# A hybrid attention, mLSTM and Hyena block on one core: new numbers in the estimate that orders TensorE's work

## The chip, the core and the metric

One NeuronCore of a Trainium2 chip runs the whole program: TensorE (PE in the rows) multiplies, VectorE (DVE), ScalarE (ACT) and GpSimd (POOL) work element by element, SyncE (SP) issues most transfers. The metric is the device time of one execution in microseconds. Each engine works through its own list of instructions in order and waits where an operand is not there yet.

## What is computed

Two layers, each of three mixers that read one projected input; the second layer does not update the context rows.

```python
def _layer(x, ctx, c, c_ctx, w_ada, ...):
    mod = jax.nn.silu(c) @ w_ada + b_ada            # shift, scale, gate
    h = _rmsnorm(x, g_pre) * (1.0 + scale) + shift  # 1024 rows; ctx has 256 more
    qa, ka, va, za, qm, km, vm, om, zm, gm, vh, x1h, x2h, zh = _split_cols(h @ w_in)
    o_na = _neighbourhood_attention(...)             # 8 heads, softmax over a window and the context
    h_lat, h_ctx = _mlstm_bidirectional(...)         # 4 heads, chunks with a carried state
    o_hy = _hyena(...)                               # two long convolutions by FFT
    y = concatenate([o_na * silu(za), sigmoid(om) * h_lat * silu(zm), o_hy * silu(zh)]) @ w_out
    return x + gate * _rmsnorm(y, g_post)
```

All arrays are float32. The kernel splits an operand of the large products into a high and a low part (names ending in hi and lo, h and l), so that one product is three matrix products.

## The kernel before, in words

Everything TensorE does is written by Python generators, called streams. A stream for each mixer emits its matmuls stage by stage and yields in between; one stream, `projections` (rank 2, the last to be chosen), emits the products of the input with `w_in`, 34 blocks of 128 columns and the gates per layer, each block in pieces of 512, 512 and 256 rows, each piece as 24 matmuls (names `pj`). The projections depend on little, so they are the filler: `flow` takes, at each step, the first stream by rank that is ready by the estimate, and where no mixer is ready it emits three `pj` matmuls.

What counts as ready is decided by class `Clock`. It keeps a planned time `now` for TensorE, and for every instruction that the kernel emits on another engine, and for every transfer, it books a planned duration on that engine (`run`) and notes when the result is there (`done`). A stream that yields tiles is not taken before their planned time plus 0.1 plus `margin` (0.3). So the order of TensorE's list is written out by this estimate; the order on the other engines is then made by the scheduling layer below, which follows the order in which instructions were emitted and lets nothing overtake a wait within an engine or within SP's queue. The estimate has no part in the running program.

The names the text needs. In the start: `htp` transposes the normed input, `tap`, `fs` make filters. Hyena (`h1`, `h2`, `h3`, `h4`: four products of the long convolution with stores to memory and loads back between them; `ztp`, `ctp` transposes; `c1`, `c2` the context's short convolution). mLSTM (`vtp`, `gtp`, `ktp` transposes, `mc`, `mst`, `mxe`, `mpi`, `mpn`, `mto`). Then neighbourhood attention, NA: 8 heads of 5 units (4 in layer 1). A unit is scores (`apl`, `apc`), a row maximum on DVE, exponentials on ACT, scaling on POOL and DVE (tile `ae`), transposes (`apt`), copies (`ph`), and, for two units together, the product with the values (`apo`); `avt` transposes values. Four `work` streams take units in turn. The loads of a head are `ark`, `arq` (keys, queries), `av` (values) and `ab` (bias, three buffers). In the names of instructions the first number is the layer, for NA then head and unit: `apl0_6_1` is layer 0, head 6, unit 1.

Last, `w_out`. `out_early` starts when the layer's projections or its NA are finished, in the memory that the projections' input gives free: it loads eight blocks (`wos`, 512 KB each, four buffers), splits them into `woh` (ACT) and `wol` (POOL, or POOL and DVE in turn once NA is over), and while NA is not finished it multiplies seven of the eight blocks for up to four row tiles (names `op`). `out_proj` does the rest, and for layer 0 its results are normed and transposed for the next layer (`htp1`).

Of the kernel before, what the change touches and what calls it, by code (L numbers as in the profile page):

```python
# [13 lines left out]
F32 = mybir.dt.float32  # L14
# [3 lines left out]
ALU = mybir.AluOpType  # L18
# [28 lines left out]

class Clock:

    RATE = dict(vector=(0.07, 1 / 960), scalar=(0.08, 1 / 1200), gpsimd=(0.2, 1 / 480))  # L50

    def __init__(self):
        self.now = 0.0
        self.runs, self.wrote, self.used, self.slots, self.home = {}, {}, {}, {}, {}

    @staticmethod
    def region(ap):
# [14 lines left out]
    def ready(self, aps):  # L72

        t = 0.0
        for ap in aps:
            name, r0, r1, c0, c1 = self.region(ap)
            for a0, a1, b0, b1, w in self.wrote.get(name, ()):
                if w > t and a0 <= r1 and r0 <= a1 and b0 <= c1 and c0 <= b1:
                    t = w
        return t  # L80

    def slot(self, ap):

        t = ap.tensor
        if ap.space == DRAM:
            return 0.0
        if t.name not in self.home:
            taken = self.slots.setdefault(t.tag, [])
            free = 0.0
            if len(taken) < t.tag_meta.bufs:  # L90
                taken.append(t.name)
            else:
                i = min(range(len(taken)), key=lambda i: self.used.get(taken[i], 0.0))
                free = self.used.get(taken[i], 0.0)
                taken[i] = t.name
            self.home[t.name] = free
        return self.home[t.name]
# [34 lines left out]
    def issue(self, engine, op, args, kw):  # L132
        outs = [kw[k] for k in ("out", "accum_out") if isinstance(kw.get(k), bass.AP)] or [args[0]]
        ins = [x for x in list(args) + list(kw.values()) if isinstance(x, bass.AP) and not any(x is o for o in outs)]
        t = max([self.now, self.ready(ins + [o for o in outs if o.space != DRAM])] + [self.slot(o) for o in outs])
        n = max(math.prod(x.shape[1:]) for x in outs + ins)
        if op == "dma_start":
            t = self.run("queue", 0.5, t + 0.2)
            end = self.run("dma", max(0.05, math.prod(outs[0].shape) * 4 / 360e3), t + 0.6) + 0.9
        else:  # L140
            fixed, per = self.RATE[engine]
            end = self.run(engine, fixed + n * per, t + 0.1)
        self.done(outs, ins, end)

# [16 lines left out]
class Kern:  # L161
# [16 lines left out]

    def mm(self, o, lhsT, rhs, start, stop, beside=False):

        n = 0 if beside else max(math.prod(o.shape[1:]), 128) * 4 if lhsT.dtype == F32 else max(math.prod(o.shape[1:]), 256)
        self.nc.tensor.matmul(o, lhsT=lhsT, rhs=rhs, start=start, stop=stop)  # L182
        self.pe(max(n / 2400.0, 0.06), o, [lhsT, rhs])

    def tr(self, out, in_, identity):
        self.nc.tensor.transpose(out=out, in_=in_, identity=identity)  # L186
        self.pe(out.shape[1] / 1200.0, out, [in_])

    def announce(self, what):
# [1851 lines left out]
```

## Time and profile before

| what | value |
|---|---|
| median of three runs | 1971.73 us (1970.43 to 1983.2) |
| the profiled execution | 1979.88 us, span 1978.0 us |
| PE busy | 1827.2 us, 92% of the span |
| granted TensorE clock, mean of the span | 0.968 |
| DVE, ACT, POOL busy | 53%, 39%, 23% |

PE is the engine that is nearly always busy. What is not its work is the time in which it is idle (151 us in all) and the time in which its clock is granted at half. Both are read by stage, since each stage has other waits.

### The profile page before, as it was taken

The page shows a single profiled execution, that of the slowest core. Times are in us where ns is not written, and L with a number is a line of the kernel's source. Part 1 is how long each engine was busy: PE and PEld are TensorE (multiplying, and loading weights), DVE is VectorE, ACT ScalarE, POOL GpSimd, SP SyncE. Part 2 cuts the span into 40 slices and gives each one's busy share as a digit, 9 for nine tenths or more (in the row PEclk, how much of TensorE's full clock was granted, in tenths as well). Part 3 has the DMA queues.
Part 4 walks back from the last instruction along what each step waited for, and adds up shares of the span by engine and source line. Part 5 has one row for each costly group of instructions (what it writes and reads, how often), then busy time and mean ns, then how long its engine had stood idle before and what let it go on. Part 6 is the DMA issues. An engine that isn't in the chain of part 4 may idle for free.

```text
span 1978.0 us, 28234 instructions
## 1 busy us (share of the span) xinstructions
PE 1827.2 (92%) x10008; PEld 1444.0 (73%) x10008; DVE 1054.5 (53%) x2402; ACT 780.2 (39%) x1517; POOL 457.7 (23%) x368
## 2 busy tenths in 40 slices
PE   8699988998999899999988998899899989999898
PEld 2365867787788677788877876678677767887776
DVE  3744353537735366677545534344762457777433
ACT  3645342414323244555343443332323145554321
POOL 1534120313220111212131123122412111222300
PEclk9799999999999999999998999899899999999999
DMA  8476887863221667655253457764222565554443
GB/s 314 140 246 219 277 229 229 232 231 97 89 81 46 197 188 217 206 163 160 96 189 98 148 170 209 205 195 168 77 79 82 156 196 146 161 170 132 159 148 107
DMA packets 233674, 328.91 MB, mean 166 GB/s; under 512 B 22573, under 2 KB 162249, under 8 KB 231614
## 3 DMA queue, kind: packets, MB, share of 16 engines
q1 hardware_dynamic: 182398, 247.67, 41.2%
q10 hardware_dynamic: 51136, 79.45, 11.8%
q8 instruction: 79, 1.29, 0.3%
q14 instruction: 61, 0.50, 0.1%
HBM read 230.82 MB, written 96.21 MB: 165 GB/s over the span
## 4 chain that ended last, share of the span: by engine, by line
PE 38%; DMA 6%; DVE 5%; issue 5%; ACT 2%; POOL 1%; SPq 0%; ACTq 0%; POOLq 0%; DVEq 0%
PE pj L182 15%; PE op L182 10%; PE apo L182 3%; PE apt L186 2%; PE h L182 2%; PE apl L182 1%; DMA wos<-in_wout 1%; PE apc L182 1%; DMA raw<-pr 1%; DVE u L155 1%; DMA pr<-sr 1%; PE mpn L182 1%; PE avt L186 1%; ACT ae L155 0%; POOL usw L155 0%
## 5 line engine op out<-in xcount | busy, mean ns | idle before, releaser
L182 PE MATMUL pj<-hhi,wh 128*128 128x512 f32 (+2 forms) x1504 | 599.4, 399 | 8.0 <-ACT sv L155 6.2
L182 PE MATMUL pj<-hlo,wh 128*128 128x512 f32 (+2 forms) x1504 | 554.1, 369 | 0.1
L182 PE MATMUL pj<-hhi,wl 128*128 128x512 f32 (+1 forms) x1456 | 538.8, 370 | 0.0
L182 PEld LDWEIGHTS pj<-hhi,wh 128*128 128x128 f32 (+1 forms) x1504 | 288.6, 192 | 61.7 <-issue 14.9
L182 PEld LDWEIGHTS pj<-hlo,wh 128*128 128x128 f32 (+1 forms) x1504 | 288.7, 192 | 47.6 <-issue 9.5
L182 PEld LDWEIGHTS pj<-hhi,wl 128*128 128x128 f32 x1456 | 280.3, 193 | 47.0
L155 POOL TENSOR_TENSOR wl<-wr,wh 128x1024 fp32r<-128x1024 f32 x68 | 163.7, 2407 | 547.9 <-ACT wh L155 473.0
L155 POOL TENSOR_SCALAR ae<-ae,ast 128x640 f32<-128x640 f32 (+1 forms) x72 | 68.2, 948 | 405.4 <-DVE ast L155 359.4
L155 ACT ACTIVATE ae<-ae,ast 128x640 f32<-128x640 f32 (+1 forms) x144 | 113.1, 787 | 85.6 <-DVE ast L155 82.2
L182 PE MATMUL op<-woh,yh 128*128 128x512 f32 x288 | 115.9, 402 | 8.9 <-ACT yh L155 8.9
L186 PE MATMUL apt<-ident,ae 128*128 128x128 f32 x672 | 101.8, 278 | 17.9 <-ACT ph L155 5.3
L182 PE MATMUL op<-woh,yl 128*128 128x512 f32 x288 | 114.4, 397 | 0.3 <-DVE yl L155 0.3
L182 PE MATMUL op<-wol,yh 128*128 128x512 f32 x288 | 114.6, 398 | 0.0
L155 ACT CAST wh<-wr 128x1024 fp32r<-128x1024 f32 (+1 forms) x70 | 71.9, 1028 | 102.3 <-PE pj L182 84.2
L155 ACT COPY sr<-pj 128x512 f32<-128x512 f32 (+3 forms) x94 | 49.2, 524 | 149.4 <-PE pj L182 141.7
L186 PEld LDWEIGHTS apt<-ident,ae 128*128 128x128 f32 x672 | 80.3, 142 | 33.8 <-issue 7.1
L155 ACT COPY ph<-apt 128x512 f32<-128x512 f32 (+1 forms) x136 | 65.0, 482 | 87.2 <-PE apt L186 82.3
L155 DVE CUSTOM_DVE_ANT_0 ae<-apl,ab 128x384 f32<-128x384 f32 x128 | 69.0, 552 | 36.2 <-PE apl L182 21.0
L182 PE MATMUL apo<-ph,aVn 128*64 128x256 f32 (+1 forms) x800 | 80.9, 350 | 0.4 <-ACT ph L155 0.4
L182 PEld LDWEIGHTS apo<-ph,aVn 128*64 128x64 f32 x800 | 51.9, 137 | 29.0 <-issue 8.8
L182 PEld LDWEIGHTS op<-woh,yh 128*128 128x128 f32 x288 | 55.7, 194 | 20.8 <-ACT yh L155 9.5
L155 DVE TENSOR_TENSOR yl<-gr,yh 128x1024 fp32r<-128x1024 f32 (+1 forms) x22 | 24.5, 1113 | 78.2 <-ACT yh L155 78.1
(255 smaller groups left out, 3058.6 us busy)
## 6 DMA issues: line engine op xcount, KB each, us to landing
wr<-in_wblk SPq DMA_DIRECT2D x68, 512.0 KB
ab<-in_nab SPq DMA_DIRECT2D x96, 192.0 KB
pr<-sr ACTq DMA_DIRECT2D x64, 256.0 KB
k<-ks SPq DMA_DIRECT2D x128, 128.0 KB
wada<-in_wada ACTq DMA_DIRECT2D x32, 512.0 KB
raw<-pr SPq DMA_DIRECT2D x20, 512.0 KB
ark<-pr SPq DMA_DIRECT2D x32, 320.0 KB
wada<-in_wada SPq DMA_DIRECT2D x16, 512.0 KB
```

What stands on the lines that cost most here:

```text
L155: r = emit(*args, **kw)
L182: self.nc.tensor.matmul(o, lhsT=lhsT, rhs=rhs, start=start, stop=stop)
L186: self.nc.tensor.transpose(out=out, in_=in_, identity=identity)
```

## The change

Only the numbers in `Clock` and the way it books a few things change. Fixed times of the vector, scalar and gpsimd engines go from 0.07, 0.08, 0.2 to 0.155, 0.165, 0.25 us, with an extra for results that are summed aside (`accum_out`) and for powers; a matmul is planned 9% longer (`PASS`), at least 0.12 us, and 0.15 us are added when the part of the array that is used changes (`turn`, `MODE`). A transfer ends 1.6 instead of 0.9 us after its bytes, at 300, 180 or 90 instead of 360 GB/s by the length of its rows, and a transfer that ACT issues takes planned time of ACT.

```diff
--- before.py
+++ after.py
@@ -47,11 +47,19 @@
 
 class Clock:
 
-    RATE = dict(vector=(0.07, 1 / 960), scalar=(0.08, 1 / 1200), gpsimd=(0.2, 1 / 480))
+
+    RATE = dict(vector=(0.155, 1 / 960, 0.08), scalar=(0.165, 1 / 1200, 0.19), gpsimd=(0.25, 1 / 478, 0.0))
+    POW = 0.3
+
+    PASS, MODE = 1.09, 0.15
+
+    LATENCY = 0.6, 1.6
+    SPEED = ((2048, 300e3), (512, 180e3), (0, 90e3))
 
     def __init__(self):
         self.now = 0.0
         self.runs, self.wrote, self.used, self.slots, self.home = {}, {}, {}, {}, {}
+        self.mode = None
 
     @staticmethod
     def region(ap):
@@ -78,6 +86,19 @@
                 if w > t and a0 <= r1 and r0 <= a1 and b0 <= c1 and c0 <= b1:
                     t = w
         return t
+
+    @staticmethod
+    def inner(ap):
+
+        run, out = 1, []
+        for stride, n in reversed(list(ap)):
+            if n == 1:
+                continue
+            if stride != run:
+                break
+            out.append((stride, n))
+            run *= n
+        return out
 
     def slot(self, ap):
 
@@ -135,10 +156,16 @@
         t = max([self.now, self.ready(ins + [o for o in outs if o.space != DRAM])] + [self.slot(o) for o in outs])
         n = max(math.prod(x.shape[1:]) for x in outs + ins)
         if op == "dma_start":
-            t = self.run("queue", 0.5, t + 0.2)
-            end = self.run("dma", max(0.05, math.prod(outs[0].shape) * 4 / 360e3), t + 0.6) + 0.9
+            t = self.run("queue" if engine == "sync" else engine, 0.4, t + 0.2)
+            row = 4 * min(math.prod(n for s, n in self.inner(x.ap)) for x in outs[:1] + ins[:1])
+            speed = next(v for k, v in self.SPEED if row >= k)
+            end = self.run("dma", max(0.05, math.prod(outs[0].shape) * 4 / speed), t + self.LATENCY[0]) + self.LATENCY[1]
         else:
-            fixed, per = self.RATE[engine]
+            fixed, per, side = self.RATE[engine]
+            if "accum_out" in kw:
+                fixed += side
+            if ALU.pow in kw.values():
+                fixed += self.POW
             end = self.run(engine, fixed + n * per, t + 0.1)
         self.done(outs, ins, end)
 
@@ -178,12 +205,21 @@
 
     def mm(self, o, lhsT, rhs, start, stop, beside=False):
 
-        n = 0 if beside else max(math.prod(o.shape[1:]), 128) * 4 if lhsT.dtype == F32 else max(math.prod(o.shape[1:]), 256)
+        n = 0 if beside else max(math.prod(o.shape[1:]), 128) * 4 if lhsT.dtype == F32 else max(math.prod(o.shape[1:]), 256) * Clock.PASS
         self.nc.tensor.matmul(o, lhsT=lhsT, rhs=rhs, start=start, stop=stop)
-        self.pe(max(n / 2400.0, 0.06), o, [lhsT, rhs])
+        self.turn(lhsT.shape[0], math.prod(lhsT.shape[1:]))
+        self.pe(max(n / 2400.0, 0.06 if beside else 0.12), o, [lhsT, rhs])
+
+    def turn(self, rows, columns):
+
+        mode = [next(s for s in (32, 64, 128) if n <= s) for n in (rows, columns)]
+        if self.clock.mode not in (None, mode):
+            self.clock.now += Clock.MODE
+        self.clock.mode = mode
 
     def tr(self, out, in_, identity):
         self.nc.tensor.transpose(out=out, in_=in_, identity=identity)
+        self.turn(in_.shape[0], math.prod(in_.shape[1:]))
         self.pe(out.shape[1] / 1200.0, out, [in_])
 
     def announce(self, what):
```

Every engine keeps the same work (TensorE's list has 7664 rows in both); what moves is the order. How many `pj` matmuls stand in TensorE's list ahead of some places:

| first instruction of | before | change |
|---|---|---|
| Hyena, layer 0 (h10_0_0_0) | 408 | 480 |
| mLSTM, layer 0 (vtp0_0_0) | 915 | 1212 |
| NA, layer 0 (apl0_0_0_0) | 1704 | 1992 |
| NA head 5, layer 0 (apl0_5_0_0) | 2058 | 2430 |
| NA head 7, layer 0 (apl0_7_0_0) | 2223 | 2496, all of the layer |
| Hyena, layer 1 (h11_0_0_0) | 2613 | 2616 |
| mLSTM, layer 1 (vtp1_0_0) | 3102 | 3249 |
| NA, layer 1 (apl1_0_0_0) | 3813 | 3936 |
| NA head 7, layer 1 (apl1_7_0_0) | 4239 | 4428, of 4464 |

Between mto0_1_2 and apl0_0_0_0 stand 111 `pj` before and 96 in the change; between mto1_1_1 and apl1_0_0_0 102 and 75.

TensorE's list in layer 1 around h41_0_0_0, the last product of the first long convolution, before:

```order
L182 MATMUL h31_1_0_1_11053<-pa1_1_0_1_10953,d2i_1_10481 128x512
L182 MATMUL pj1_31_0_11024<-hhi1_9506,wh1_31_10898 128x512
L182 MATMUL pj1_31_0_11024<-hlo1_9507,wh1_31_10898 128x512
L182 MATMUL pj1_31_0_11024<-hhi1_9506,wl1_31_10899 128x512
L182 MATMUL h21_1_0_3_11068<-t11_1_0_10769,d2_1_10479 128x512
L182 MATMUL pj1_31_0_11024<-hhi1_9506,wh1_31_10898 128x512
L182 MATMUL pj1_31_0_11024<-hlo1_9507,wh1_31_10898 128x512
L182 MATMUL pj1_31_0_11024<-hhi1_9506,wl1_31_10899 128x512
L182 MATMUL pj1_31_0_11024<-hhi1_9506,wh1_31_10898 128x512
L182 MATMUL pj1_31_0_11024<-hlo1_9507,wh1_31_10898 128x512
L182 MATMUL pj1_31_0_11024<-hhi1_9506,wl1_31_10899 128x512
L182 MATMUL h41_0_0_0_11083<-m1i_1_10477,s21_0_0_10987 128x64 x8
```

And the same place in the change (the run of `pj` ahead of h41_0_0_0 has 18 rows, its last six are shown):

```order
L209 MATMUL pj1_18_0_11227<-hhi1_9544,wh1_18_11129 128x512
L209 MATMUL pj1_18_0_11227<-hlo1_9545,wh1_18_11129 128x512
L209 MATMUL pj1_18_0_11227<-hhi1_9544,wl1_18_11130 128x512
L209 MATMUL pj1_18_0_11227<-hhi1_9544,wh1_18_11129 128x512
L209 MATMUL pj1_18_0_11227<-hlo1_9545,wh1_18_11129 128x512
L209 MATMUL pj1_18_0_11227<-hhi1_9544,wl1_18_11130 128x512
L209 MATMUL h41_0_0_0_11246<-m1i_1_10474,s21_0_0_11146 128x64 x8
```

More projections stand between the products of the convolution: 6 directly ahead of h41_0_0_0 before, 18 in the change, and the other channel's h21 and h31 have moved ahead of them.

TensorE's list in NA of layer 0, around the transposes of head 5, unit 2, before:

```order
L182 MATMUL apc0_5_4_8130<-kl0_5_7382,qs0_5_7381 128x256
L186 MATMUL apt0_5_2_0_8156<-ident_109,ae0_5_2_0_7979 128x128
L186 MATMUL apt0_5_2_0_8156<-ident_109,ae0_5_2_1_7996 128x128
L186 MATMUL apt0_5_2_0_8156<-ident_109,ae0_5_2_0_7979 128x128
L186 MATMUL apt0_5_2_0_8156<-ident_109,ae0_5_2_1_7996 128x128
L186 MATMUL apt0_5_2_1_8162<-ident_109,ae0_5_2_0_7979 128x128
L186 MATMUL apt0_5_2_1_8162<-ident_109,ae0_5_2_1_7996 128x128
L186 MATMUL apt0_5_2_1_8162<-ident_109,ae0_5_2_0_7979 128x128
L186 MATMUL apt0_5_2_1_8162<-ident_109,ae0_5_2_1_7996 128x128
L182 MATMUL pj0_32_1024_8168<-hhi0_373,wh0_32_7461 128x256
L182 MATMUL pj0_32_1024_8168<-hlo0_374,wh0_32_7461 128x256
L182 MATMUL pj0_32_1024_8168<-hhi0_373,wl0_32_7462 128x256
```

And in the change:

```order
L221 MATMUL apt0_5_2_0_8720<-ident_109,ae0_5_2_0_8457 128x128
L221 MATMUL apt0_5_2_0_8720<-ident_109,ae0_5_2_1_8471 128x128
L209 MATMUL apl0_6_0_1_8734<-kh0_6_8231,qs0_6_8229 128x384
L209 MATMUL apl0_6_0_1_8734<-kl0_6_8230,qs0_6_8229 128x384
L209 MATMUL apc0_6_0_8710<-kh0_6_8231,qs0_6_8229 128x256
L209 MATMUL apc0_6_0_8710<-kl0_6_8230,qs0_6_8229 128x256
L221 MATMUL apt0_5_2_1_8750<-ident_109,ae0_5_2_0_8457 128x128
L221 MATMUL apt0_5_2_1_8750<-ident_109,ae0_5_2_1_8471 128x128
L221 MATMUL apt0_5_2_1_8750<-ident_109,ae0_5_2_0_8457 128x128
L221 MATMUL apt0_5_2_1_8750<-ident_109,ae0_5_2_1_8471 128x128
L221 MATMUL apt0_5_2_2_8756<-ident_109,ae0_5_2_0_8457 128x128
L221 MATMUL apt0_5_3_0_8765<-ident_109,ae0_5_3_0_8546 128x128
```

In the change the layer's last `pj` stands in unit 5_0, and from there to the first `op` (op0_0_0, directly after the first scores of unit 7_1) TensorE's list holds NA alone, some 8 units of it. Before, the first `op` of layer 0 stands behind the whole of NA and behind 156 more `pj`; in the change three tiles of `op` stand among the last units. In layer 1 the last `pj` stands ahead of apt1_6_3_1, and the first `op` directly behind apo1_7_1; before, both stand behind all of NA.

SP's queue where the loads of `w_out` of layer 0 are issued, in the change:

```order
L182 DMA wos0_0_8606<-in_wout 128x1024
L182 DMA wos0_1_8608<-in_wout 128x1024
L182 DMA yp0_83<-so0_25_1024_8596 128x256
L182 DMA wos0_2_8610<-in_wout 128x1024
L182 DMA wos0_3_8612<-in_wout 128x1024
L182 DMA wos0_4_8630<-in_wout 128x1024
L182 DMA wos0_5_8645<-in_wout 128x1024
L182 DMA av0_5_2_8671<-pr0_10_5219 64x2x128 x2
L182 DMA arq0_7_8705<-pr0_3_5562 64x1280 x2
L182 DMA wos0_6_8728<-in_wout 128x1024
L182 DMA wos0_7_8732<-in_wout 128x1024
L182 DMA av0_5_3_8781<-pr0_10_5219 64x2x128 x2
```

Before, the eight `wos` stand together behind NA's last load. In the change NA's loads av0_5_2, arq0_7, av0_5_3 and, next, the bias ab0_6_4 stand behind `wos` issues that need a buffer back. POOL's list has there ae0_5_3, wol 0 and 1, ae0_5_4, wol 2 to 4, ae0_6_0, wol 5 to 7; layer 1 has the same pattern around units 7_1 to 7_3.

## Rows read from the trace of the kernel before

**Rows 1.** The page: busy us, share of span and instructions of each engine

```profile
PE 1827.2 (92%) x10008; PEld 1444.0 (73%) x10008; DVE 1054.5 (53%) x2402; ACT 780.2 (39%) x1517; POOL 457.7 (23%) x368
```

**Rows 2.** Stretches by stage: start:end, length, busy us (instructions) by engine, clock, DMA

```profile
0.00:100.00 100.00, 73.72 (x261) 33.68 (x262) 58.23 (x126) 52.63 (x106) 37.25 (x36) 0.88 0.63 224
...
257.00:442.00 185.00, 170.22 (x927) 136.91 (x926) 77.94 (x122) 58.16 (x95) 41.68 (x36) 0.98 0.79 229
442.00:655.00 213.00, 201.56 (x1163) 165.92 (x1162) 131.53 (x294) 72.74 (x160) 51.98 (x29) 0.98 0.24 82
655.00:700.00 45.00, 35.42 (x191) 28.21 (x189) 13.48 (x33) 10.44 (x17) 5.87 (x3) 0.89 0.75 226
700.00:885.00 185.00, 174.74 (x1250) 141.93 (x1252) 125.27 (x400) 96.39 (x202) 35.72 (x32) 0.98 0.68 198
...
1003.00:1054.00 51.00, 38.03 (x153) 31.48 (x154) 22.96 (x37) 18.45 (x36) 10.55 (x9) 0.80 0.46 150
...
1152.00:1360.00 208.00, 192.72 (x951) 150.98 (x949) 74.90 (x98) 68.93 (x108) 50.00 (x52) 0.96 0.71 206
1360.00:1558.00 198.00, 185.74 (x1008) 151.71 (x1008) 117.35 (x256) 63.57 (x138) 53.72 (x30) 0.97 0.25 83
...
1601.00:1866.00 265.00, 255.67 (x1646) 210.47 (x1646) 175.78 (x517) 129.09 (x255) 59.21 (x43) 0.99 0.52 157
```

**Rows 3.** PE's waits in 257:442 (us in total, times, longest), by what ended them

```profile
PE h L182 <- DVE pa L155: 5.0, 5, 2.6
...
PE c L182 <- DMA fc<-in_fcw: 3.2, 1, 3.2
```

**Rows 4.** Timeline of PE: start, length, instructions, idle time before and its end

```profile
689.12 0.69 PE L182 MATMUL apl<-kh,qs 128*128 128x384 f32 x1 [4.43 <-DVE qs L155]
...
702.39 0.60 PE L186 MATMUL apt<-ident,ae 128*128 128x128 f32 x4
...
1040.59 1.97 PE L186 MATMUL htp<-ident,xr 128*128 128x128 f32 x8 [5.15 <-DVE xr L155]
...
1207.28 2.05 PE L182 MATMUL h<-pa,d2i 128*128 128x128 f32 x4 [4.85 <-issue]
...
1239.72 3.02 PE L182 MATMUL h<-m1i,s 128*128 128x64 f32 x16 [2.98 <-DMA s<-d2s]
...
1879.76 0.80 PE L182 MATMUL op<-woh,yh 128*128 128x512 f32 x1 [6.30 <-ACT yh L155]
```

**Rows 5.** Chain that ended last: start, us, what (a run of 42 projections)

```profile
1479.62 9.57 PE pj L182 x42
```

**Rows 6.** NA under full filler, and two sparse stretches, as in rows 2

```profile
860.00:977.00 117.00, 116.21 (x807) 97.20 (x806) 79.20 (x247) 60.09 (x132) 24.83 (x21) 1.00 0.42 126
66.00:87.00 21.00, 13.10 (x45) 9.41 (x45) 16.48 (x36) 16.32 (x39) 8.29 (x9) 0.51 0.28 84
1039.00:1053.00 14.00, 8.74 (x29) 7.13 (x30) 9.90 (x18) 6.21 (x14) 3.09 (x3) 0.51 0.47 152
```

**Rows 7.** Groups in 860:977: count, busy us, mean ns, idle before

```profile
L182 PE MATMUL pj<-hlo,wh 128*128 128x512 f32 x65 | 25.5, 392 | 0.0
...
L182 PE MATMUL pj<-hlo,wh 128*128 128x256 f32 x37 | 10.4, 282 | 0.0
...
L155 POOL TENSOR_SCALAR ae<-ae,ast 128x640 f32<-128x640 f32 (+1 forms) x17 | 15.3, 901 | 80.1 <-DVE ast L155 73.2 <-PE apc L182 6.4 <-PE apt L186 0.5
L155 DVE SCALAR_TENSOR_TENSOR sz<-sz,pj 128x512 f32<-128x512 f32 (+1 forms) x11 | 6.5, 589 | 1.3 <-ACT sz L155 1.0
```

**Rows 8.** The loads of w_out: groups, and the timeline of the first

```profile
L155 POOL TENSOR_TENSOR wol<-wos,woh 128x1024 fp32r<-128x1024 f32 x8 | 21.4, 2672 | 27.4 <-DMA wos<-in_wout 19.8 <-ACT woh L155 7.5
...
983.70 14.51 SPq L155 DMA_DIRECT2D wos<-in_wout  x8
...
989.30 1.05 ACT L155 CAST woh<-wos 128x1024 fp32r<-128x1024 f32 x1 [5.02 <-DMA wos<-in_wout]
```

## The prediction

> **What bounds the kernel now.** I read the page first: PE is busy for 1827.2 of 1978.0 us [rows 1], so no other engine can be the bound over the whole, and what a new order can win is PE's idle time, 151 us, and the time at the half clock. The second view is the table of stretches by stage [rows 2]: length less PE's busy time is a stage's idle time, and length times (1 less the clock) is what the half clock costs it. The reader is to see that the loss has three kinds of place. (a) The start, 0 to 100 us: 26.3 us idle, clock 0.88; there is hardly filler yet. (b) Stages of chains with filler at hand: Hyena of layer 0 (257 to 442) idles 14.8 us and loses 3.7 to the clock, its mLSTM (442 to 655) 11.4 and 4.3, the start of NA (655 to 700) 9.6 and 5.0, NA up to 885 10.3 and 3.7; in layer 1 Hyena 15.3 and 8.3, mLSTM 12.3 and 5.9, NA's body 9.3 and 2.7 [rows 2]. (c) Where layer 0 ends (1003 to 1054): 13.0 and 10.2. The third view, PE's waits and the timeline with what ended each wait, shows what the estimate misses in (b): long convolutions wait for a load, a DVE product or a round trip through memory, 3.2 us for fc, 4.85 for a pa, 2.98 for s [rows 3, 4]. Filler existed; it stood behind the waiting instruction.
>
> **The change part by part.** It adds and removes no instruction. Its new durations cost nothing on the chip; all comes from the order. A projection costs 9.57/42 = 0.228 us of PE [rows 5], half of that with 256 columns (an estimate).
>
> *Hyena.* In layer 0 the change has 15 more projections between ctp0_0_0 and c1 (1.7 us with 256, 3.4 with 512 columns) for the wait of 3.2 [rows 3], and 33 more between h30_1_0_1 and h30_1_0_2, where the longest of the waits for pa (2.6 of 5.0 in all) ends [rows 3]. I take 10 of the 14.8 us idle as filled, and 2 of the clock's 3.7: 12 gained. In layer 1 the wait of 4.85 has 15 more ahead of it (3.4 us), that of 2.98 has 18 where 6 stood [rows 4]; I take 11 of 15.3 and half of 8.3: 15 gained. Bounds for both: half of it, and all that [rows 2] hold, 42.
>
> *mLSTM.* Ahead of its waits stand about as many as before, some 6 more ahead of vtp: 2 in layer 0, 4 in layer 1.
>
> *Start of NA.* The order gives back something here. Before, 111 projections cover the way from the end of mLSTM to the first scores, and PE still waits 4.43 us for qs [rows 4]; now 96 do, and 75 instead of 102 in layer 1. The 15 and 27 fewer are 3.4 and 6.2 us; I take 3 and 5 lost.
>
> *Body of NA.* Heads 0 to 4 get more filler: 438 projections against 354 in layer 0, 363 against 294 in layer 1. Of the idle 10.3 and 9.3 us [rows 2] I take 4 and 2 gained.
>
> *NA without filler.* More filler early means less late. Under full filler 17 units took 117 us (860 to 977, three forms of 65 and 37 projections each, all forms alike) [rows 6, 7]: 194 x 0.228 + 112 x 0.114 = 57 us are projections, so a unit costs PE (117 - 57 - 0.8)/17 = 3.5 us. DVE, 79.2 less the projections' sz 6.5, needs 4.3 us per unit. From the last projection of layer 0 to the first op stand about 8 units: 28 us of PE, 34 of DVE. On top comes SP's queue: the first wos can be issued only when the last projection frees the memory; the first cast came 5.6 us after the issue, took 1.05, and each wol takes 2.67 on POOL [rows 8]. wol 0 to 3 with one ae of 0.9 between [rows 7] end at 5.6 + 1.05 + 4 x 2.67 + 0.9 = 18.2 us; then wos 7 goes, and av0_5_3 and ab0_6_4 behind it land some 3 us later (half of the first wos; an estimate). Unit 6_1 waits for that until 21 us with 3.7 units of PE work (13 us) done. The other 4.3 follow at 4.3 us each: 40 us in all, 12 idle, and at the 0.89 of the start of NA [rows 2] 4 more: 16 lost. Bounds: 7 (DVE alone) and 31 (6.7 us per unit, half of the 13.3 us from the first scores to the first transposes, 689.12 to 702.39 [rows 4]: 53 us). In layer 1 the same chain holds avt1_7_1 until 21 us with 3 units of work there: 9 lost (bounds 4, 20).
>
> *Ends of the layers.* Before, the products with w_out start after NA and 156 more projections, PE waits for xr (5.15, 3.67 elsewhere in that stretch) and falls to half clock [rows 4, 6]. Now three tiles of op stand among the last units, tile 3 and half of tile 4 stand ahead of the first htp1: of 13.0 + 10.2 I take 18 gained. In layer 1 the wait of 6.30 for yh [rows 4] and the half clock around it go: 8. Cover: op's last block comes from NA's last unit; its store and load, some 8 us, lie under 16 us of op. If the products were done early, it would be bare.
>
> *New misses.* Another order misses elsewhere: 5 lost, half of what NA's body idles (bounds 0, 10).
>
> Sum: -12 - 15 - 2 - 4 + 3 + 5 - 4 - 2 + 16 + 9 - 18 - 8 + 5 = -27 us. Against the profiled execution's 1979.88 that is 1952.9. That execution lies 8.15 us over the median of 1971.73, so the forecast is 1945 us.
>
> A row speaks against keeping the filler's end sparse: in 66 to 87, PE busy 13.1 of 21 us and mostly in transposes, and in 1039 to 1053, 8.7 of 14 us, the granted clock was 0.51, so 1.2 GHz almost throughout [rows 6]. The Trainium skill, "TensorE: Matmul & The Clock Gate", Part 4: PE-mode transpose, says that transposes do not count as PE-busy in the way matmuls do. The rows agree with it, without showing that transposes rather than idle time are the cause. [...]
>
> **The rivals.** *The gains are given back.* The filler is finite; each stall covered early is one uncovered later, and PE waits in NA as much as it waited before. For: NA starts with fewer projections. Against: with w_out's products the tail has filler again. If the hyena gains halve (13) and new misses double with a tail at its 31, the net is about -27 + 13 + 5 + 15 = +6 at worst and -9 midway: 1950 to 1978, I say 1966.
>
> *Half clock without filler.* The 28 us of PE work take up to 56 instead of 40 in all, and layer 1 loses a little: 13 more, 1958. For: the two rows at 0.51. Against: NA's start, with 35.4 of 45 us busy, kept 0.89 [rows 2].
>
> *Slower: SP's queue makes NA serial.* Loads of NA stand behind wos issues that wait for POOL, which waits for them in turn after ae. If units follow one another at 13.3 us [rows 4] instead of overlapping, 8 units take 106 instead of 40: 66 more, 2011. It decides (over 1991) from (40 + 46)/8 = 10.8 us per unit. For: the order of SP and POOL. Against: only two or three loads are held, not each.
>
> *Larger gain.* DVE alone paces the tail, no new miss, all hyena waits go: 7 instead of 16, 0 instead of 5, 42 instead of 27: -56, 1916.
>
> **How the numbers follow.** Chances: forecast 0.45, larger gain 0.10, given back 0.22, half clock 0.11, slower 0.12. The forecast's own range is 1928 to 1962. The range 1915 to 1984 leaves out the slow case and little else. A measurement of this kernel can tell about 1% from no change, so 1952 and 1991 are the marks: faster is the larger gain, 0.38 of the forecast's 0.45 and 0.05 of the others, 0.53; same 0.35; slower 0.12.
>
> **What would show it.** Hyena of layer 1 idle under 6 us and c1 without a wait: right; the same sums as before: the estimate was not what failed. A stretch in heads 5 and 6 of layer 0 with no pj, PE some two thirds busy, 40 us long, DVE over 80% busy; its clock tells the half-clock rival, and waits for ab or av with SP at a wos the slow one. htp1_0_0 without a wait of 5 us. Wrong overall if idle time in the body of NA doubles, or if the sparse stretch passes 70 us.

## The result, and the profile after

The changed kernel is not faster: its median is 1987.49 us (9 runs, 1981.61 to 1994.92) against 1971.73 (9 runs), a ratio of 1.0068 with a 95% interval of 1.004 to 1.0097. The forecast was 1945 us, its range 1915 to 1984. The profiled execution of the changed kernel took 1981.61 us. Executions of one kernel differ by up to 1.4% (1963.25 to 1989.92 us in 31 runs of before), so the verdicts below rest on the ratio to the runs of before that were made with each, and the profiles tell where the time lies.

The changed kernel by stages: stretch, length, busy us (instructions) of PE, PEld, DVE, ACT, POOL, clock, DMA share, GB/s. In order: Hyena, mLSTM, the start of NA and NA's body of layer 0; the last units with three early tiles of `op`; the end of layer 0; Hyena, mLSTM, the body of NA, its last units and the end of layer 1.

```profile
265.00:455.00 190.00, 189.01 (x1044) 155.72 (x1042) 74.17 (x107) 64.50 (x104) 43.55 (x34) 1.00 0.79 226
455.00:699.00 244.00, 231.40 (x1316) 192.42 (x1315) 138.23 (x322) 76.80 (x168) 58.30 (x37) 0.97 0.28 91
699.00:743.00 44.00, 30.59 (x185) 24.91 (x184) 15.73 (x48) 14.13 (x26) 6.71 (x4) 0.88 0.80 239
743.00:925.00 182.00, 173.11 (x1209) 138.51 (x1208) 124.01 (x360) 85.37 (x176) 35.09 (x28) 0.98 0.64 191
950.00:1048.00 98.00, 78.13 (x472) 60.93 (x470) 60.52 (x162) 46.36 (x95) 27.53 (x19) 0.88 0.36 109
1048.00:1165.00 117.00, 102.47 (x465) 82.70 (x465) 71.70 (x142) 56.35 (x125) 28.10 (x37) 0.96 0.49 159
1189.00:1374.00 185.00, 179.52 (x925) 142.73 (x924) 66.45 (x77) 62.79 (x98) 43.06 (x34) 1.00 0.69 201
1374.00:1595.00 221.00, 200.70 (x1079) 163.60 (x1079) 117.16 (x268) 66.55 (x142) 57.61 (x37) 0.94 0.27 90
1634.00:1838.00 204.00, 201.60 (x1306) 166.24 (x1305) 144.18 (x424) 104.98 (x207) 46.35 (x34) 1.00 0.56 167
1838.00:1893.00 55.00, 45.46 (x283) 34.53 (x282) 32.03 (x81) 27.85 (x50) 23.52 (x13) 0.91 0.47 148
1893.00:1979.80 86.80, 79.31 (x342) 64.04 (x342) 32.98 (x60) 17.01 (x39) 4.42 (x8) 0.97 0.40 140
```

Length less PE's busy time is idle time, and length times (1 less the clock) is what the half clock costs, as in [rows 2]. Hyena of layer 0 idles 1.0 us where it idled 14.8, that of layer 1 5.5 where it idled 15.3, both at full clock: the gain is there. But mLSTM of layer 1 idles 20.3 instead of 12.3 at a clock of 0.94 instead of 0.97, and the last units of layer 0, which had projections before (PE busy 116.21 of 117 us, [rows 6]), now idle 19.9 of 98 us at 0.88. Three long waits in PE's timeline (start, length, instruction, idle time before and what ended it):

```profile
728.80 0.69 PE L209 MATMUL apl<-kh,qs 128*128 128x384 f32 x1 [11.06 <-DVE qs L182]
1421.64 0.69 PE L221 MATMUL gtp<-ident,G 128*128 128x128 f32 x2 [9.05 <-ACT G L182]
1621.47 0.69 PE L209 MATMUL apl<-kh,qs 128*128 128x384 f32 x1 [9.16 <-DVE qs L182]
```

The wait for qs was 4.43 us in layer 0 before [rows 4]; the one at gtp is the round trip of mLSTM's gates. In layer 1 both waits were short before:

```profile
1391.85 0.62 PE L186 MATMUL gtp<-ident,G 128*128 128x128 f32 x2 [2.46 <-ACT G L155]
1587.91 0.45 PE L182 MATMUL apl<-kh,qs 128*128 128x384 f32 x1 [0.93 <-DVE qs L155]
```

### The profile page after: what moved, and what is told of

The parts are those of the page before. It is cut to its first block, busy times and chain, and to the rows that moved or that the text cites. A ratio compares the mean times of both kernels' runs of the same rounds, so it can differ in the third digit from the quotient of the medians.

```text
span 1979.8 us, 28227 instructions
## 1 busy us (share of the span) xinstructions
PE 1824.0 (92%) x10008; PEld 1437.3 (73%) x10008; DVE 1046.0 (53%) x2398; ACT 782.8 (40%) x1521; POOL 477.4 (24%) x376
## 3 DMA queue, kind: packets, MB, share of 16 engines
q10 hardware_dynamic: 51136, 79.45, 11.5%
## 4 chain that ended last, share of the span: by engine, by line
PE 51%; DVE 9%; DMA 5%; issue 3%; ACT 3%; POOL 2%; SPq 0%; DVEq 0%; POOLq 0%; ACTq 0%
PE pj L209 25%; PE op L209 7%; PE apo L209 4%; PE apt L221 3%; PE h L209 2%; PE apl L209 2%; PE mpn L209 2%; DMA arq<-pr 1%; PE apc L209 1%; DVE ae L182 1%; DVE u L182 1%; PE mxe L209 1%; DVE ast L182 1%; PE mpi L209 1%; PE mst L209 1%
## 5 line engine op out<-in xcount | busy, mean ns | idle before, releaser
L209 PEld LDWEIGHTS pj<-hlo,wh 128*128 128x128 f32 (+1 forms) x1504 | 284.7, 189 | 50.5 <-issue 12.8
L221 PE MATMUL apt<-ident,ae 128*128 128x128 f32 x672 | 106.4, 284 | 25.6 <-ACT ph L182 6.8
L209 PE MATMUL op<-woh,yh 128*128 128x512 f32 x274 | 111.0, 405 | 2.6 <-ACT ops L182 1.6
L209 PE MATMUL op<-woh,yl 128*128 128x512 f32 x274 | 107.9, 394 | 0.9 <-DVE yl L182 0.9
L209 PE MATMUL op<-wol,yh 128*128 128x512 f32 x274 | 107.8, 393 | 0.0
L209 PE MATMUL apl<-kh,qs 128*128 128x384 f32 x128 | 52.2, 408 | 29.0 <-DVE qs L182 20.2
L182 ACT ACTIVATE mE<-mxe,gnat 128x128 f32<-128x128 f32 x144 | 40.9, 374 | 59.1 <-PE mxe L209 46.7
```

The costliest lines, as they stand in the source:

```text
L182: r = emit(*args, **kw)
```

## Experiments

**The order of before once more.** All new numbers set back (those of the engines, the least time of a matmul and the booking of transfers likewise).

```diff
-    PASS, MODE = 1.09, 0.15
+    PASS, MODE = 1.0, 0.0
...
```

> The changed file with all its new numbers set back to the old ones: TensorE's order is that of the kernel before. A second profile of that order: the profiled execution of before lies 8 us over the median of its runs, so differences between two traces may be 8 us off what the times say. If the stalls are a property of the order, every stage's idle time and clock loss comes out within 3 us of the first profile; what differs by more is chance.

One execution, 1970.88 us, 9 less than the first profile. Hyena of layer 0, then Hyena and mLSTM of layer 1 in this profile:

```profile
255.80:432.20 176.40, 164.86 (x918) 132.07 (x917) 79.96 (x118) 60.05 (x97) 38.68 (x32) 0.99 0.81 233
1154.00:1342.00 188.00, 174.84 (x885) 136.66 (x884) 70.62 (x88) 66.55 (x104) 46.20 (x44) 0.99 0.74 215
1342.00:1549.00 207.00, 194.07 (x1068) 159.03 (x1068) 119.11 (x266) 65.90 (x141) 59.70 (x37) 0.98 0.28 91
```

In layer 1 idle time comes out near [rows 2], 13.2 and 12.9 us for 15.3 and 12.3; the clock's loss does not, 1.9 us in Hyena instead of 8.3. Hyena of layer 0 idles 11.5 us instead of 14.8 and loses 1.8 to the clock instead of 3.7. So some 6 us of the clock's loss in layer 1, of which the prediction booked half as won, and 5 us in layer 0 were chance of one execution.

**Which numbers move Hyena's projections.** Without those of transfers (360 GB/s and 0.9 us behind again):

```diff
-            t = self.run("queue" if engine == "sync" else engine, 0.4, t + 0.2)
...
+            t = self.run("queue", 0.5, t + 0.2)
...
```

> The new durations of the engines and of TensorE, the old ones of transfers: Hyena has 322 and 367 projections (before 337 and 394; changed 516 and 520), no unit of NA is without projections, 111 and 129 are left after NA. If the gain in Hyena comes from the transfers' numbers, Hyena idles here as before, 14 to 18 us with 4 to 9 of clock loss. Theory F (finite projections): the ends of both layers cost what they cost before, and the kernel stands within 8 us of before, 1965 to 1980.

1.0035 [1.0005, 1.0065], 1980.69 us, within 8 us of its runs of before as theory F expects. Hyena of layer 0 and 1:

```profile
251.00:415.00 164.00, 149.28 (x824) 117.99 (x823) 73.78 (x106) 55.93 (x90) 36.18 (x31) 0.98 0.84 235
1180.00:1338.00 158.00, 148.29 (x748) 114.80 (x748) 65.05 (x80) 55.29 (x87) 37.07 (x32) 0.98 0.76 218
```

14.7 us idle again in layer 0; in layer 1 9.7, where 14 to 18 were expected and the changed kernel has 5.5. What covers Hyena are the transfers' numbers, in layer 1 only in part.

Without the engines' fixed times:

```diff
-    RATE = dict(vector=(0.155, 1 / 960, 0.08), scalar=(0.165, 1 / 1200, 0.19), gpsimd=(0.25, 1 / 478, 0.0))
+    RATE = dict(vector=(0.07, 1 / 960, 0.0), scalar=(0.08, 1 / 1200, 0.0), gpsimd=(0.2, 1 / 480, 0.0))
...
```

> The new numbers of transfers and of TensorE, the old ones of the other engines: Hyena has 518 and 520 projections as in the changed kernel, NA of layer 0 has 4 units without any instead of 8 and 78 early products instead of 114; mLSTM of layer 1 has only 60 ahead of gtp1, and 27 projections are left after its NA. Theory F: Hyena's gain stays (idle under 3 and 7 us), the end of layer 0 costs 25 to 40 us instead of 51; what mLSTM of layer 1 lacks (42 x 0.228 = 9.6 us) is added to the wait at gtp1. In all 1970 to 1985. If the engines' fixed times are what makes the order bad, it is faster than before, under 1965.

1.0104 [1.0068, 1.014], 1995.53 us, worse than expected. Hyena idles 5.8 and 8.8 us in this profile, a little over what was expected. The end of layer 0 is better than expected: its last units and its end (the first two rows) idle 10.9 and 5.1 us, 21 with the clock. Layer 1 is worse: its mLSTM and its end (the last two) idle 32.8 and 25.9.

```profile
945.00:1031.00 86.00, 75.09 (x500) 59.27 (x499) 57.00 (x160) 44.60 (x91) 28.85 (x18) 0.94 0.45 137
1031.00:1144.00 113.00, 107.92 (x511) 88.19 (x510) 70.12 (x140) 57.16 (x126) 27.80 (x37) 1.00 0.50 164
1357.00:1565.00 208.00, 175.22 (x949) 142.74 (x948) 120.92 (x266) 61.91 (x135) 56.13 (x35) 0.91 0.27 84
1870.00:1992.00 122.00, 96.11 (x411) 77.67 (x410) 46.60 (x69) 28.70 (x53) 14.95 (x12) 0.90 0.44 149
```

**New numbers in Hyena alone.** A switch, `fresh`, takes all old numbers after Hyena.

```diff
+            fixed, per, side = (self.RATE if self.fresh else self.BEFORE)[engine]
...
+        self.clock.fresh = False
         with tc.tile_pool(name=f"ml{l}", bufs=1, side=side) as pool:
```

> The changed kernel with the new durations only until the end of Hyena in each layer, the old ones for mLSTM, NA and the ends of the layers. Hyena has the changed kernel's 516 and 520 projections, NA of layer 0 has 4 units without projections instead of 8, layer 1 none, and there are 78 + 381 projections instead of 102 + 420 ahead of gtp1 and in mLSTM of layer 1. Theory F (finite projections): Hyena keeps its gain (idle about 1 and 5.5 us), the stretch without projections loses about half of 33 us, and the kernel is at 1955 to 1970, faster than before and than the changed one. A theory that any gain in Hyena is given back later in full: 1970 to 1985.

1.0097 [1.0059, 1.0135], 1991.35 us: a miss. Hyena kept its gain (idle 1.4 and 6.4 us). The old numbers, started from another state, gave another order in layer 1. PE's waits there:

```profile
1406.36 0.69 PE L226 MATMUL gtp<-ident,G 128*128 128x128 f32 x2 [11.76 <-ACT G L187]
1881.38 0.80 PE L214 MATMUL op<-woh,yh 128*128 128x512 f32 x1 [16.77 <-ACT yh L187]
```

gtp1 has 156 projections ahead of it since the last product of Hyena, where before had 177; and no projection is left to cover the load of w_out. So the order of a stage was not kept when only the stage ahead of it changed.

**More units without projections.** TensorE's numbers set back:

```diff
-    PASS, MODE = 1.09, 0.15
+    PASS, MODE = 1.0, 0.0
...
```

> The new durations without those of TensorE (no 9% on a pass, no 0.15 us for a change of array use): the estimate thinks projections shorter, so it spends more of them early: 23 units of NA without projections in layer 0 and 11 in layer 1, instead of 8 and 2. Theory F: each unit without them costs about 4 us of TensorE's time (33 us for 8), less what early products of w_out cover: 40 to 90 us slower than the changed kernel, 2028 to 2078. A theory that the loss lies at the end of NA whatever the count of units (w_out's splits and loads, the last units' chain): within 15 us of the changed kernel, 1975 to 2003.

1.0193 [1.0148, 1.0237], 2008.79 us, between the two theories. The first row is the stretch of layer 0 from the last projection to the first early product, with most of the 23 units; the next two are NA's body (its first 80 us still have projections) and the last units with early products, the fourth is NA's body in layer 1.

```profile
868.60:1017.60 149.00, 110.96 (x823) 82.79 (x821) 120.93 (x368) 85.06 (x178) 44.08 (x33) 0.89 0.64 190
789.00:960.00 171.00, 142.92 (x1025) 110.39 (x1025) 129.08 (x376) 89.88 (x182) 48.63 (x34) 0.92 0.71 211
984.00:1064.00 80.00, 71.89 (x460) 55.27 (x457) 50.33 (x160) 38.89 (x88) 10.60 (x12) 0.96 0.32 93
1657.00:1882.00 225.00, 202.66 (x1280) 165.26 (x1281) 156.57 (x461) 116.05 (x224) 63.83 (x42) 0.95 0.58 171
```

The first row idles 38.0 us and loses 16 to the clock; in the changed kernel the stretch between the same places (54.30 us, shown below) idles 18.4 and loses 12. Units without projections cost, but not in proportion to their count: the changed kernel's 8 are dear for another reason too, which the next run shows.

**w_out's split off GpSimd.**

```diff
-            (nc.vector if i % 2 and f"N{l}" in self.known else nc.gpsimd).tensor_tensor(out=wl[:, b, :], in0=raw[i], in1=wh[:, b, :].bitcast(F32), op=ALU.subtract)
...
+                self.tc.nc.scalar.copy(wl[:, b, :], raw[i])
...
```

> The changed kernel with the split of w_out's low part taken off GpSimd: ScalarE copies the raw block into wol instead (so the products with wol are not the reference's; this is left out), and the estimate is charged as before, so TensorE's order is that of the changed kernel. Theory P (a DVE instruction that reads SBUF stands until the GpSimd instruction beside it ends): the tiny DVE operations on ast, 1.6 to 2.3 us under wol in the changed kernel, take 0.16 us again; of the 9.3 us that DVE stood under wol in the stretch without projections most comes back, and the kernel is 6 to 12 us faster than the changed one (1976 to 1982 by the medians). Theory F (what costs is that no projections are left, and DVE's own work paces the units): the tiny operations get short as well, but the stretch keeps its length within 3 us, 1985 to 1990.

1.0051 [1.003, 1.0072], 1984.18 us. DVE, then POOL, in the changed kernel:

```profile
952.60 1.58 DVE L182 TENSOR_SCALAR ast<-ast 128x2 f32<-128x2 f32 x1
957.92 1.63 DVE L182 TENSOR_TENSOR ast<-ast 128x2 f32<-128x2 f32 x1
959.58 2.27 DVE L182 TENSOR_SCALAR ast<-ast 128x2 f32<-128x2 f32 x1
```

```profile
949.44 4.71 POOL L182 TENSOR_TENSOR wol<-wos,woh 128x1024 fp32r<-128x1024 f32 x2 [1.80 <-ACT woh L182]
957.17 6.98 POOL L182 TENSOR_TENSOR wol<-wos,woh 128x1024 fp32r<-128x1024 f32 x3 [0.25 <-ACT woh L182]
```

The first ends at 954.18, POOL's pair at 954.15; the others at 959.55 and 961.85, where the first and second of POOL's three (6.98/3 = 2.33 us each) end by this reckoning, 959.50 and 961.82. Without POOL's splits the same kind of operation:

```profile
954.07 0.16 DVE L182 TENSOR_SCALAR ast<-ast 128x2 f32<-128x2 f32 x1
955.91 0.14 DVE L182 TENSOR_TENSOR ast<-ast 128x2 f32<-128x2 f32 x1
```

The stretch from the last projection to the first `op`, in the changed kernel and (second fence) here:

```profile
944.80:999.10 54.30, 35.93 (x223) 27.68 (x221) 41.09 (x101) 31.21 (x62) 24.87 (x16) 0.78 0.56 173
```

```profile
946.80:993.90 47.10, 32.61 (x224) 24.84 (x221) 32.06 (x101) 38.34 (x70) 6.55 (x8) 0.86 0.63 200
```

DVE's busy time for the same 101 instructions falls by 9.0 us, the stretch by 7.2. Locally theory P holds. The time moves by 3 us, inside the intervals, where theory P had 6 to 12: in layer 1, with the copies on ScalarE, the last units took 3.4 us longer (58.8 for 55.4).

**w_out held back until NA is over.**

```diff
-        yield {f"P{l}", f"N{l}"}
+        yield f"N{l}"
```

> The changed kernel with the work on w_out (its loads, its splits, the products of three tiles ahead of NA's end) held back until NA is over; the projections stand where the changed kernel has them, 8 units of NA without any in layer 0, 2 in layer 1. Theory P, and a theory that the loads on SP's queue disturb NA: the 8 units get shorter by 10 us or more (about 58 us instead of 68 to the last scores); what is lost after NA is the 26 us of products that stood under it. Theory F: the 8 units stay as long within 5 us, and the kernel loses 15 to 30 us against the changed one, 2002 to 2017.

1.0147 [1.0113, 1.018], 2001.54 us. The last units, and the end of layer 0:

```profile
952.00:1017.00 65.00, 50.81 (x352) 36.52 (x353) 53.90 (x163) 43.14 (x88) 19.37 (x15) 0.92 0.47 146
1017.00:1168.00 151.00, 130.91 (x594) 107.94 (x589) 72.75 (x141) 58.71 (x128) 28.23 (x37) 0.92 0.41 130
```

98 us less 114 early products (26 us) would be 72 us; the units took 65, again 7 us less, without splits and loads beside them. But the end grew from 117 to 151. So starting early was right: by the ratios it is worth 0.8%.

**Fewer early products.**

```diff
-        for tt in range(4):
+        for tt in range(1 if upd else 4):
```

> The changed kernel with the early products of w_out in layer 0 cut from 114 to 42 (one tile instead of three); projections and units stand as in it. From the end of NA's last unit to the first long convolution's last h it took 117 us in the changed kernel, 115 where 48 products had been done early and 113 with 78. Theory E (the end of the layer has a chain of its own of some 115 us, whatever PE has left to do): the 72 products (16.4 us) fit into its idle 14.5 us: the end stays at 115 to 120 us, the stretch of units gets shorter by 8 to 14, and the kernel is 6 to 14 us faster than the changed one, 1974 to 1981. Theory W (PE's work counts; early products are won time): the end grows by 16 us, the stretch of units shrinks by as much or less, 1986 to 1994.

1.0019 [0.9996, 1.0042], 1982.89 us.

```profile
953.00:1038.00 85.00, 63.48 (x399) 48.50 (x398) 57.70 (x160) 43.41 (x90) 27.15 (x19) 0.84 0.38 114
1038.00:1165.00 127.00, 118.80 (x547) 97.70 (x548) 71.57 (x143) 58.32 (x128) 27.86 (x37) 0.97 0.48 151
```

The units got 13 us shorter, the end 10 longer, for 16.4 us of products moved: in the profile neither theory is clean. The times speak for a part of E: with ratios of 1.0019 and 1.0068, whose intervals just meet, doing those 72 products early had won nothing that can be seen.

**Rationing the projections in NA of layer 0.** One number, while that stage is ordered:

```diff
...
+            self.clock.PASS = 1.4 if upd else Clock.PASS
             yield from self.na(l, pool, upd)
+            self.clock.PASS = Clock.PASS
```

> The changed kernel with one number different, and only while NA of layer 0 is ordered: a pass of TensorE is reckoned at 1.4 instead of 1.09, so fewer projections go ahead of each unit there. Hyena and mLSTM of layer 0 and all of layer 1 are the changed kernel's. 4 units are without projections instead of 8, 30 products of w_out come early instead of 114. Theory F (what the changed kernel loses in layer 0 is the stretch that has no projections left): from the first scores to the next layer's first convolution it takes 10 to 22 us less than the changed kernel's 460 us, and the time is 1966 to 1978. A theory that the units cost the same wherever the projections stand (the loss comes from w_out's loads and the chain behind NA): within 5 us of the changed kernel.

0.9958 [0.9931, 0.9984], 1966.2 us: as theory F expects, 1.1% under the changed kernel. The last units and the end of layer 0:

```profile
941.00:1018.00 77.00, 67.03 (x454) 52.84 (x452) 55.39 (x158) 43.42 (x90) 28.90 (x19) 0.91 0.48 145
1018.00:1145.00 127.00, 120.26 (x560) 99.21 (x558) 72.12 (x139) 58.09 (x127) 28.27 (x37) 0.97 0.49 154
```

10.0 + 6.7 us idle for 19.9 + 14.5, with the same splits and loads in it, 4 bare units instead of 8 and 30 early products instead of 114. With 1.6:

```diff
...
+            self.clock.PASS = 1.6 if upd else Clock.PASS
...
```

> As the run with 1.4, with a pass at 1.6: no unit of layer 0 is without projections, 57 are left after NA, and no product of w_out comes early; its loads and splits stand behind NA under 57 projections (13 us), before under 156. Theory F: the units lose nothing at their end, but the products wait for w_out's load and the end of the layer costs 20 to 40 us as in the kernels whose loads came after NA; about the changed kernel or up to 10 us faster, 1977 to 1990. If only the units without projections counted, it would be the fastest of the three, under 1970.

1.0059 [1.0034, 1.0084], 1989.13 us, as expected. No unit is bare, but `op` is:

```profile
1024.52 0.79 PE L209 MATMUL op<-woh,yh 128*128 128x512 f32 x1 [16.02 <-ACT yh L182]
```

Of the three runs the one in which projections last almost to NA's end, and no longer, is the fastest.

**The gates of mLSTM in layer 1.** Weights' splits taken off GpSimd:

```diff
-        nc.gpsimd.tensor_tensor(out=wlo, in0=wr, in1=whi.bitcast(F32), op=ALU.subtract)
+        self.tc.nc.scalar.copy(wlo, wr)
...
```

> The changed kernel with the split of every projection's weights taken off GpSimd: ScalarE copies the raw weights into wl (the products with wl are not the reference's; this is left out), the estimate charged as before, so TensorE's order is the changed kernel's. Theory P (DVE instructions that read SBUF stand until the GpSimd instruction beside them ends): in the gates of mLSTM in layer 1 the scans take 0.87 us again instead of 3.06 and the pair on u 2.6 instead of 4.78; the wait of 9.05 at gtp1 gets 3 us or more shorter, and the kernel 5 to 15 us faster than the changed one. Theory Q (the chain of the gates is set by its loads, by SP's order and ScalarE; DVE waits anyway): within 3 us at gtp1, and the time the same or, with 71 us more on ScalarE, longer.

0.9972 [0.9948, 0.9995], 1970.59 us, 17 under the changed kernel. DVE in the gates there, in the changed kernel, here and (third fence) before:

```profile
1395.02 3.06 DVE L182 TENSOR_TENSOR_SCAN G<-G 40x128 f32<-40x128 f32 x2
1409.94 4.78 DVE L182 SCALAR_TENSOR_TENSOR u<-raw,cols,u 128x1024 f32<-128x1024 f32 x2
```

```profile
1397.29 0.86 DVE L182 TENSOR_TENSOR_SCAN G<-G 40x128 f32<-40x128 f32 x2
1409.81 2.60 DVE L182 SCALAR_TENSOR_TENSOR u<-raw,cols,u 128x1024 f32<-128x1024 f32 x2
```

```profile
1369.70 0.87 DVE L155 TENSOR_TENSOR_SCAN G<-G 40x128 f32<-40x128 f32 x2
1387.84 2.61 DVE L155 SCALAR_TENSOR_TENSOR u<-raw,cols,u 128x1024 f32<-128x1024 f32 x2 [1.32 <-ACT u L155]
```

PE there, and its mLSTM of layer 1 as a stretch:

```profile
1419.34 0.69 PE L221 MATMUL gtp<-ident,G 128*128 128x128 f32 x2 [4.97 <-ACT G L182]
```

```profile
1377.00:1587.00 210.00, 198.73 (x1077) 162.52 (x1076) 111.75 (x268) 76.18 (x153) 31.59 (x26) 0.96 0.28 95
```

The wait at gtp1 is 4.1 us shorter and the stage idles 11.3 us instead of 20.3. From the start of these scans to that gtp it takes 26.6 us in the changed kernel, 22.1 here and 22.2 before. Theory P.

More projections ahead of gtp1 instead:

```diff
-        yield 9.0
+        yield (9.0, 14.0)[l]
```

> The changed kernel with one constant in mLSTM of layer 1: 14 instead of 9 us are reckoned for the gates' round trip. It puts 123 instead of 102 projections ahead of gtp1 (21 x 0.228 = 4.8 us) and 399 instead of 420 behind it; all else stands as in the changed kernel. Theory L (idle time is local: what is covered stays won while there are projections): the waits of 9.05 and 1.68 us at gtp1 fall by about 4.8 and some half clock goes with them, 1978 to 1984. Theory G (gains are given back in the same layer): the wait falls, but mLSTM or NA's end of layer 1 loses as much, 1985 to 1990.

1.0030 [1.0, 1.0059], 1981.17 us; the wait of 9.05 is 4.31, as theory L expects. The time is 6 us lower, with intervals that overlap.

**Do the gains add?** Layer 0 without the engines' numbers, 16 us for the gates of layer 1:

```diff
...
-        yield 9.0
+        yield (9.0, 16.0)[l]
...
+        self.clock.fresh = l > 0
```

> Layer 0 with the new numbers of transfers and TensorE and the old ones of the other engines (there its idle time and clock loss came to about 74 us from the first long convolution to the next layer, against 103 in the changed kernel and 84 before), layer 1 with all new numbers and 16 instead of 9 us for the gates. Theory S (each stage's loss depends on the order of that stage alone, so they add): 43 us at the start + 74 + 82 of layer 1, less 7 at the gates = 192 of loss, the changed kernel's 227 less 35: 1947 to 1960. Theory G (what is covered in one stage comes back in another): no better than before, 1970 to 1990.

0.9958 [0.9942, 0.9975], 1965.27 us: 22 of the expected 35 us under the changed kernel. Layer 0 won nearly what it should (80 us lost between the same places, 74 expected); mLSTM of layer 1 won nothing, idle 20.4 us. With 24 more projections in front than in the changed kernel the wait moved to one of them:

```profile
1409.55 0.58 PE L211 MATMUL pj<-hhi,wh 128*128 128x256 f32 x1 [7.59 <-ACT sv L184]
```

Its PSUM bank is emptied by copies `sv` on DVE and ACT, which stand behind the gates' own operations there. So the filler can have to wait too.

And ten instead of two us for layer 1's first scores:

```diff
-                yield from self.want("s", qs, kh, kl, extra=2.0)
+                yield from self.want("s", qs, kh, kl, extra=2.0 if turn else (2.0, 10.0)[l])
```

> As the combination above (layer 0 without the engines' numbers, 16 us for the gates in layer 1), and 10 instead of 2 us reckoned for the first scores of layer 1, which puts 114 instead of 93 projections ahead of them (4.8 us). Theory S: the wait of 9 us for qs there falls by about 4.8 and some half clock goes: 2 to 7 us faster than the combination without it, 1942 to 1956. Theory G: within 2 us of it.

0.9949 [0.9925, 0.9973], 1967.85 us. The wait for qs, 9.16 us in the changed kernel and 7.76 in the combination, was 0.82; the time did not fall by what the runs can tell. The order behind it changed too: 78 early products in layer 1 instead of 42, the last units took 66.1 us for 55.9 and the end 80.6 for 86.9. This run settles nothing.

Rationing and the 14 us for the gates together (both diffs above):

> The run with 1.4 in NA of layer 0, and 14 instead of 9 us reckoned for the gates in layer 1 (which alone brought the changed kernel from 1.0068 to 1.003 of the time before). If losses of separate stages add: 5 to 8 us under the run with 1.4 alone, 1960 to 1972, faster than before and than the changed kernel. If they don't: as the run with 1.4.

0.9924 [0.989, 0.9959], 1960.37 us: faster than before and than the changed kernel, by 0.8 and 1.4%, and 6 us under rationing alone, as expected, though the intervals of these two overlap.

## Why the prediction was wrong

**Right.** Hyena: 17.5 us won by the rows in layer 0 (190 - 189.01 at full clock, against 14.8 + 3.7) and 18 in layer 1, forecast 12 and 15. Some of that is luck: against the second execution of the old order it is 12 and 10. NA's start: 13.4 + 5.3 for 9.6 + 5.0, 4 lost, forecast 3; in layer 1 the wait for qs went from 0.93 to 9.16 us and about 5 were lost, as forecast. NA's body in layer 0: 8.9 + 3.6 for 10.3 + 3.7, forecast 4 won, measured 1.5. In layer 1 the body idles 2.4 us in 204 (10 won, forecast 2) and the last units lose 9.5 + 5.0 (forecast 9, bound 20): together 5 lost, forecast 7. The end of layer 1 loses 7.5 + 2.6 us, and 14.4 + 5.6 before: 10 won, forecast 8. Two of its signs came as foretold: Hyena of layer 1 idles under 6 us and PE waits at no product of the context's convolution (c1), and PE in the bare stretch is two thirds busy (35.93 of 54.30 us). DVE there is 76% busy, not over 80%, and the stretch 54 us long, not 40.

**NA without filler, forecast 16, measured 19.9 + 11.8 = 32.** The step that failed is the price of a unit, 4.3 us by DVE, 40 us for 8. The work was rightly sized: DVE needs 32.06 us for them when alone, forecast 34. But it was taken from a stretch without `wol` (POOL 24.83 of 117 us, [rows 6]). Under `wol` DVE took 41.09, and the stretch 54.3, where the prediction's upper bound had 53. `wol` had been reckoned only as a delay of loads. 7.2 of the 14.3 us are shown to be POOL's; the rest stays unsplit between units that follow one another and the clock of 0.78, forecast at 0.89. At 6.8 us per unit the stretch is as long as with the 6.7 of the upper bound.

**The end of layer 0, forecast 18 won, measured 4.** 14.5 + 4.7 are still lost in 1048 to 1165. The prediction named the risk itself: products done early leave the last chain bare. It looked only at the store and load of NA's last block (8 us under 16 us of `op`). The waits for xr, which it took as gone with the wait of 5 us, stayed. PE's waits in 1048 to 1165 (us in total, times, longest) make up all of the 14.5 us:

```profile
PE htp L221 <- DVE xr L182: 10.5, 4, 4.3
PE op L209 <- DVE xr L182: 4.0, 3, 3.0
```

From NA's last unit to the last `htp1` it took 113 to 117 us with 48, 78, 108 or 114 products done before, and 127 with 30 or 42, where PE idled only 6.7 and 8.2 us. What sets those 113 us, and why DVE is late with xr, was not tried.

**mLSTM, forecast 6 won, measured 4 lost in layer 0 and 15 in layer 1.** Counting projections ahead (some 6 more at vtp) was not enough, since the gates' chain itself got longer in layer 1. Its DVE operations stood under POOL's splits of weights: without these, 9.0 us of the idle time and some half clock are gone, and the chain is as short as before. That the order before met fewer of them (its second pair of scans took 0.87 us, its pair on u 2.61) is a reading of one profile each; a shorter pair of scans, of gsb, took 2.11 us before and 0.36 in the changed kernel. For layer 0 nothing was tried.

**The rivals.** "Given back" named the outcome but not its mechanism, and the time lies above its range (1950 to 1978) too. Filler did run out, but the loss was not forced: the run with 1.4 keeps Hyena's order and all of layer 1, moves projections within NA, and wins 21 us. "SP's queue makes NA serial" fell: PE's waits in the bare units were for DVE and ACT, not loads. The two longest:

```profile
956.19 0.44 PE L221 MATMUL apt<-ident,ae 128*128 128x128 f32 x2 [3.20 <-ACT ph L182]
...
977.37 0.69 PE L209 MATMUL apl<-kh,qs 128*128 128x384 f32 x1 [3.62 <-DVE ast L182]
```

"Half clock" came true in part: 0.78 over the bare stretch, not 0.5.

Counted as in the prediction, the three failed terms are 16 + 14 + 25 = 55 us. The others together came out some 14 us better than forecast: 9 in Hyena, 4 in NA and at the end of layer 1, 5 for new misses that no other stage shows, less 4 at NA's start and in its body of layer 0. 55 - 14 = 41 us is almost the distance from 1945 to 1987. That it closes so well is partly luck: by this count the loss rose by some 14 us, while the spans of the two profiled executions differ by 1.8 us (1978.0 and 1979.8) and the medians by 16.

## What to carry to other kernels

A better estimate of one stage's waits moves filler out of another; before trusting it, ask where the filler now ends, and reserve some for the last stage that needs it: here one number that rations it was worth 1.1%. An operation on GpSimd is not free: in this kernel some VectorE operations on operands in SBUF stood beside it until it ended. Price a stretch with the instructions that will be there, not with those that were. And a second profile of the unchanged kernel tells cheaply which of its losses are chance.

## What the runs showed of the hardware

VectorE operations of 0.16 us on 128x2 elements took 1.58 to 2.27 us beside GpSimd's subtraction of 1024 columns and ended with it to 0.03 or 0.05 us; a pair of scans took 3.06 for 0.86 without the splits. The Trainium skill, "SBUF — State Buffer", section "Who interferes with whom", says that VectorE shares a pair of ports with GpSimd, that instructions with two SBUF inputs or in a 2-port mode need it, and that the loser waits for the whole instruction; the trace agrees for `ast`, with these numbers. It shows a longer time for the scan too, which that section does not name. The clock's loss of the same order differed between two executions, 8.3 and 1.9 us in Hyena of layer 1, with idle times of 15.3 and 13.2.
